# Modulation chunks summed over 1024 columns per VectorE operation, in pieces of 512 KB

## The chip, the cores and the metric

One core of one Trainium2 chip runs the kernel. The metric is device time in microseconds, the median of the timed runs. The engines are named as in the profile: PE is TensorE's matmul, PEld its weight load, DVE is VectorE, ACT is ScalarE, POOL is GpSimd, SP is the engine that issues most transfers.

## The reference, cut to what matters

The program is one layer of a hybrid backbone with width 2048 on 128 context tokens and 128 latent tokens, side by side as 256 columns:

```python
mod_ctx = (silu(c_ctx) @ w_mod + b_mod)      # 6 * 2048 values for the context tokens
mod_lat = (silu(c)     @ w_mod + b_mod)      # and 6 * 2048 for the latent tokens
shift1, scale1, gate1, shift2, scale2, gate2 = split(mod, 6)
h = rmsnorm(x) * (1 + scale1) + shift1
# h @ w_in feeds three branches: hgrn2 (a), chunk MLP (b), gated delta-net (c)
merged = g_a * (o_a @ w_br_hg) + g_b * (o_b @ w_br_cm) + g_c * (o_c @ w_br_gdn)
x = x + gate1 * (merged @ w_out)
h2 = rmsnorm(x) * (1 + scale2) + shift2
x = x + gate2 * (square(relu(h2 @ w_ff1)) @ w_ff2)
y = rmsnorm(x)
```

The modulation is a vector-matrix product, for two vectors, with a weight matrix of 2048 x 12288 fp32 values (96 MB). The kernel calls the six parts chunks 0 to 5. Chunks 0 and 1 are needed at the start; chunk 2 (`gate1`) after the output projection, chunks 3 and 4 at the second norm, chunk 5 (`gate2`) at the end.

## The kernel before

**The main stream.** All large products go through PE in units of one weight tile `[128, 1024]`, 512 KB each (`run_stream`, L388). SP loads a unit into a `raw` tile, ACT casts it to the high half `wh`, DVE subtracts to get the low half `wl` (`split`, L382), and PE multiplies three times: high by high, low by high, high by low. There are three `wh`/`wl` pairs in the steady state, so a split is made two units ahead of its use. Products accumulate in the PSUM banks `pb`; a block of 16 units gives four banks, which ACT or DVE empties.

**Fillers.** Everything else (normalizations, the three branches' inner work, modulation) is written as generators, the fillers. While it records the program, the kernel keeps a clock for each engine from a table of costs (`Meter.cost`, L123), and after each few matmuls `pump` (L300) lets fillers place their next instructions. A filler gets its turn when DVE and ACT are no more than `MARGIN` = 1.8 us ahead of PE by that clock. Small matmuls of fillers use the banks `pf` and stand between the main stream's. The recorded order is final: each engine runs its instructions in the order in which they were placed, and waits where an input is late. `finish` (L342) forces fillers out where the main stream needs their results; `gate` (L1451) calls it ahead of its evacuation for the branches that must be done by then, `gmlp` (L1337) among them for the second branch's gates. `norm_gate` (L787) closes the first and the third branch.

**The modulation.** Chunks 0 and 1 go through PE at the start. Chunks 2 to 5 are the background filler `mods` (L725), the last in the list, which gets a turn when DVE is less than `BG` = 0.8 us ahead of PE (L312). It puts output columns on the partitions: a piece of weights `mraw` is `[128, 512]`, 256 KB, with 512 of the 2048 inputs for 128 output columns. `cb` holds the matching quarter (`kq`) of both input vectors, copied to all partitions by a POOL transfer from the DRAM tile `csd`. For each of the two vectors one `scalar_tensor_tensor` multiplies the piece by `cb`, and its accumulated sum goes to one column of `part` (L757). Sixteen pieces make one quarter of a chunk; then `part` is added to `modc` (L761). There are three `mraw` buffers, and a piece is asked for two pieces ahead, on SP's queue, the same that carries the `raw` tiles. Chunk 5 starts only when the first block of `ff1` is done (`late`).

The chunks after the norm wait for `drain_mod` (L1673), which forces the background where a chunk is not complete. Tiles named `z` are large buffers that pass from one stage to the next.

Of the kernel before, what the change touches and what calls it, by code (L numbers as in the profile page):

```python
# [7 lines left out]
F32 = mybir.dt.float32  # L8
# [6 lines left out]
P = 128  # L15
D = 2048
KT = D // P
NB = 1024
# [174 lines left out]
class Backbone:  # L193
# [431 lines left out]
    def start_steps(self, first, second):  # L625
# [76 lines left out]
        for db in range(8):  # L702
            wins.append([dict(kind="call", do=lambda db=db: self.finish(self.chains[db])), first[2 * db]])
            wins += [[first[2 * db + 1]], [second[db]]]
        at = {8 * (g // 3 + 1) + (5, 7, 10)[g % 3]: w for g, w in enumerate(wins)}
        allm = sum(mods, [])
        for n in range(80):
            steps += allm[n:n + 1]
# [4 lines left out]
    def spread(self):  # L713

        nc = self.nc
        i, b = self.now(self.getbank())
        nc.tensor.transpose(b[:32, :P], self.cs.rearrange("p k v -> p (k v)"), self.ident)
        j, t = self.now(self.gettmp())
        nc.scalar.copy(t[:32, :P], b[:32, :P])
        self.putbank(i)  # L720
        self.csd = self.drp.tile([4, 8, P], F32, tag="csd", name="csd")
        nc.gpsimd.dma_start(self.csd.rearrange("a b p -> (a b) p"), t[:32, :P])
        self.puttmp(j)

    def mods(self, chs):  # L725


        nc = self.nc
        todo = [(ch, kq, n) for ch in chs for kq in range(4) for n in range(16)]
        raw, at = {}, {}  # L730

        def issue(m):
            if m < len(todo):
                ch, kq, n = todo[m]
                raw[m] = self.rawp.tile([P, 512], F32, tag="mraw", name=self.nm("mraw"))
                nc.sync.dma_start(raw[m], self.I["wmodr"][ch - 2, kq, n])
                at[m] = self.clock.dma + DMA1

        issue(0)
        issue(1)  # L740
        for m, (ch, kq, n) in enumerate(todo):
            yield 0.0
            while ch == 5 and not self.late:
                yield W
            if n == 0:
                cb = self.sp.tile([P, 4, 2, P], F32, tag="cb", name=self.nm("cb"))
                nc.gpsimd.dma_start(cb.rearrange("p a v j -> p (a v j)"), self.csd[kq].rearrange("a j -> (a j)").partition_broadcast(P))
                part = self.small(32, "part").rearrange("p (n v) -> p n v", n=16)
                yield W
            issue(m + 2)  # L750
            while not self.forced and at[m] > max(self.t["dve"], self.horizon()) + 0.2:
                yield W
            w = raw.pop(m).rearrange("p (a j) -> p a j", a=4)
            junk = self.junk.rearrange("p (v a j) -> p v a j", v=2, a=4)
            for v in range(2):
                nc.vector.scalar_tensor_tensor(out=junk[:, v], in0=w, scalar=1.0, in1=cb[:, :, v, :],
                                               op0=ALU.mult, op1=ALU.mult, accum_out=part[:, n, v:v + 1])  # L757
            if n < 15:
                continue
            c = self.modc[:, ch]  # L760
            nc.vector.tensor_tensor(out=c, in0=part, in1=self.bmod[:, ch].unsqueeze(2).broadcast_to([P, 16, 2]) if kq == 0 else c, op=ALU.add)  # L761
            if kq == 3:
                self.moddone.add(ch)


# [912 lines left out]
def _blocks(w, nb=NB):  # L1678

    k, n = w.shape  # L1680
    per = NB // nb
    w = w.reshape(k // P // per, per, P, n // nb, nb).transpose(3, 0, 2, 1, 4)
    return np.ascontiguousarray(w).reshape(n // nb, k // P // per, P, NB)


def _tail(w):

    return _blocks(w[:, :1024]), _blocks(w[:, 1024:1536], 512), _blocks(w[:, 1536:], 256)


def _cols(v):

    return v.reshape(-1, P).T


def layout(x_prompt, x_sample, c, state_hgrn, state_gdn, c_ctx, norm1_g, norm2_g, w_mod, b_mod, w_in,
           hg_lb, hg_onorm_g, cm_vnorm_g, cm_ws, cm_bs, gdn_conv, gdn_A_log, gdn_dt_bias, gdn_onorm_g,
           w_br_hg, w_br_cm, w_br_gdn, w_out, w_ff1, w_ff2, final_g):
    f = np.float32
    x = np.concatenate([x_prompt[0], x_sample[0]], 0)  # L1700
    A = {}
    A["xT"] = x.T.reshape(KT, P, 256).transpose(1, 0, 2)
    A["cvec"] = np.stack([_cols(c_ctx), _cols(c[0])], 2).reshape(P, 32)
    A["par"] = np.concatenate([b_mod[0].reshape(96, P).T, _cols(norm1_g[0]), _cols(norm2_g[0]), _cols(final_g),
                               _cols(hg_lb[0].reshape(-1)), hg_onorm_g[0][:, None], gdn_onorm_g[0][:, None],
                               _cols(cm_vnorm_g[0]),
                               gdn_conv[0].reshape(9, 24, P).transpose(2, 1, 0).reshape(P, 216),
                               np.zeros((P, 16), f)], 1)
    i = np.arange(P)
    A["ident"] = np.eye(P, dtype=f)  # L1710
    le, ge = i[:, None] <= i[None], i[:, None] >= i[None]
    lt, gt = i[:, None] < i[None], i[:, None] > i[None]
    A["tri"] = np.stack([le, ge, lt, gt], 1).astype(f)
    hm = np.zeros((P, 7, P), f)
    for j in range(7):
        m = 1 << j
        hm[:, j] = (i[:, None] // (2 * m) == i[None] // (2 * m)) & (i[:, None] // m != i[None] // m)
    A["hmask"] = hm
    A["sel"] = np.tile(np.eye(2, dtype=f), (2, 1))
    A["rows"] = np.concatenate([gdn_A_log[0].reshape(-1), gdn_dt_bias[0].reshape(-1)])  # L1720
    A["bs"] = cm_bs[0].reshape(-1)
    A["wsT"] = cm_ws[0].transpose(2, 0, 1)
    A["s0hg"] = state_hgrn[0, 0].transpose(2, 0, 1, 3)
    A["s0gd"] = state_gdn[0, 0].transpose(2, 0, 1, 3)
    wm = w_mod[0]
    m2 = wm[:, :2 * D].reshape(8, 2, P, 2, 8, 256)
    A["wmods"] = m2.transpose(4, 0, 2, 1, 3, 5).reshape(8, 8, P, NB)
    A["wmodr"] = wm[:, 2 * D:].reshape(4, 512, 4, KT, P).transpose(2, 0, 3, 4, 1)
    wi = w_in[0]

    o = {"hq": 0, "hi": 1024, "hgo": 2048, "hff": 3072, "hfb": 4096, "cu": 5120, "cv": 6144, "q": 7168, "k": 8192,
         "v": 9216, "ggo": 10240, "ab": 11264, "gates": 11296}
    starts = [o[n] for n in ("hi", "hff", "hff", "hq", "hgo", "q", "k", "v", "ggo", "cu", "cv")]
    starts += [o["gates"] + NB * j for j in range(6)]
    A["win"] = np.stack([wi[:, s:s + NB].reshape(KT, P, NB) for s in starts])
    hb = wi[:, o["hfb"]:o["hfb"] + NB].reshape(8, 2, P, 2, 512)
    A["winh"] = hb.transpose(3, 0, 2, 1, 4).reshape(2, 8, P, NB)
    A["wab"] = wi[:, o["ab"]:o["ab"] + 32].reshape(2, 8, P, 32).transpose(0, 2, 1, 3).reshape(2, P, 256)
    A["wbr"] = np.stack([_blocks(w[0]) for w in (w_br_hg, w_br_cm, w_br_gdn)])
    A["wouta"], A["woutb"], A["woutc"] = _tail(w_out[0])  # L1740
    A["wff1"] = _blocks(w_ff1[0])
    A["wff2"] = np.stack([_blocks(w_ff2[0][2048 * g:2048 * g + 2048]) for g in range(3)])
    A["wff2a"], A["wff2b"], A["wff2c"] = _tail(w_ff2[0][6144:])
    return {k: np.ascontiguousarray(v) for k, v in A.items()}
# [21 lines left out]
```

## Time and profile before

| | us |
|---|---|
| timed runs: median (lowest to highest) | 2031.3 (2029.57 to 2036.58) |
| the profiled execution | 2035.48 |
| its span, first to last instruction | 2033.7 |

```profile
## 2 busy tenths in 40 slices
PE   5999999999999989998999999899999999999997
...
DVE  6876898979878986877888856577887554455565
...
mraw<-in_wmodr SPq DMA_DIRECT2D x256, 256.0 KB, 4.0
...
cb<-csd POOLq DMA_DIRECT2D x16, 512.0 KB, 5.0
```

The page cuts the span into 40 slices of some 51 us; a digit is an engine's busy share in tenths. The last two lines count transfers with their size and the median time from issue to landing. In the tables by stretch further down, each engine has its busy time in that stretch with the number of its instructions, and then come the clock that TensorE was granted, the share of the DMA engines' time in use, and GB/s. In lists in order of time, the bracket is the idle time before an instruction and what ended it. Nearly all instructions carry line L169, that of the recording helper, so they are told apart by the names of their tiles.

### The profile page before, as it was taken

What the parts mean: (1) busy time and instruction counts of PE and PEld (TensorE: products, weight loads), DVE (VectorE), ACT (ScalarE), POOL (GpSimd) and SP (SyncE); (2) the same over time, 40 slices, a digit from 0 to 9 for tenths busy, and PEclk for the clock granted to TensorE, in tenths of its full rate; (3) what the DMA queues carried; (4) which work ended last, traced back from release to release, by engine and by line L of the source; (5) the groups of instructions that cost most, each with busy time, mean ns of one, the idle gap of its engine ahead of it and who ended that gap; (6) DMA issues with size and microseconds to landing.
All of it is one profiled execution on the core that took longest, in us unless ns stands there. A gap on an engine that the chain in (4) does not pass through costs nothing.

```text
span 2033.7 us, 35303 instructions
## 1 busy us (share of the span) xinstructions
PE 1967.6 (97%) x13749; PEld 1811.8 (89%) x13749; DVE 1489.7 (73%) x2662; ACT 1018.3 (50%) x1474; POOL 47.6 (2%) x117
## 2 busy tenths in 40 slices
PE   5999999999999989998999999899999999999997
PEld 3779988999888879886888899899999999999997
DVE  6876898979878986877888856577887554455565
ACT  6774645476647534475344434644444443344343
POOL 0000000000000001010000000000000000000000
PEclk9999999999999999999999999899999999999998
DMA  9886666665567765775888756577787555555654
GB/s 344 317 292 226 225 207 216 219 204 176 194 200 240 250 215 199 236 228 187 275 276 295 251 197 200 175 239 252 259 269 254 182 183 186 180 183 187 213 192 135
DMA packets 143040, 455.56 MB, mean 224 GB/s; under 512 B 16249, under 2 KB 16921, under 8 KB 141849
## 3 DMA queue, kind: packets, MB, share of 16 engines
q1 hardware_dynamic: 135216, 423.96, 62.5%
q0 software_dynamic: 7360, 29.07, 4.4%
q8 instruction: 108, 1.77, 0.3%
q14 instruction: 60, 0.48, 0.1%
q10 hardware_dynamic: 296, 0.27, 0.0%
HBM read 442.74 MB, written 10.50 MB: 223 GB/s over the span
## 4 chain that ended last, share of the span: by engine, by line
PE 85%; DVE 6%; DMA 5%; ACT 2%; issue 2%; POOL 0%; SPq 0%; DVEq 0%; ACTq 0%; POOLq 0%
PE pb L169 76%; PE pf L169 9%; DVE wl L169 2%; DVE z L169 2%; DVE m L169 1%; DMA z<-in_s0gd 1%; ACT wh L169 1%; DMA raw<-in_wmods 1%; DMA raw<-in_win 1%; DMA mraw<-in_wmodr 1%; DVE junk L169 1%; ACT z L169 1%; DMA raw<-in_winh 0%; ACT tp L169 0%; DMA z<-sp 0%
## 5 line engine op out<-in xcount | busy, mean ns | idle before, releaser
L169 DVE TENSOR_TENSOR wl<-raw,wh 128x1024 fp32r<-128x1024 f32 x610 | 742.6, 1221 | 455.3 <-ACT wh L169 454.1
L169 ACT CAST wh<-raw 128x1024 fp32r<-128x1024 f32 x610 | 637.2, 1047 | 826.9 <-PE pb L169 739.5
L169 PE MATMUL pb<-Hh,wh 128*128 128x256 f32 x2120 | 604.6, 285 | 7.5 <-ACT Hh L169 4.7
L169 PE MATMUL pb<-Hl,wh 128*128 128x256 f32 x2120 | 601.0, 284 | 0.8 <-DVE Hl L169 0.8
L169 PE MATMUL pb<-Hh,wl 128*128 128x256 f32 x2120 | 600.7, 283 | 0.0
L169 PEld LDWEIGHTS pb<-Hh,wh 128*128 128x128 f32 x2120 | 406.3, 192 | 10.3 <-ACT Hh L169 5.2
L169 PEld LDWEIGHTS pb<-Hl,wh 128*128 128x128 f32 x2120 | 406.2, 192 | 1.5 <-DVE Hl L169 1.4
L169 PEld LDWEIGHTS pb<-Hh,wl 128*128 128x128 f32 x2120 | 406.5, 192 | 0.9
L169 PE MATMUL pb<-z,wh 128*128 128x256 f32 x2048 | 367.3, 282 | 0.0
L169 DVE SCALAR_TENSOR_TENSOR junk<-mraw,cb 128x512 bf16<-128x512 f32 x512 | 329.3, 687 | 14.6 <-DMA mraw<-in_wmodr 10.9
L169 PEld LDWEIGHTS pb<-z,wh 128*128 128x128 f32 x2048 | 317.2, 190 | 0.0
L169 PE MATMUL pb<-z,wl 128*128 128x256 f32 x1024 | 289.2, 282 | 0.1
L169 PE MATMUL pb<-wh,Hh 128*128 128x512 f32 x640 | 258.5, 404 | 3.3 <-DVE z L169 3.0
L169 PE MATMUL pb<-wl,Hh 128*128 128x512 f32 x640 | 250.4, 391 | 1.3 <-DVE wl L169 1.3
L169 PE MATMUL pb<-wh,Hl 128*128 128x512 f32 x640 | 250.3, 391 | 0.0
L169 PEld LDWEIGHTS pb<-z,wl 128*128 128x128 f32 x1024 | 195.0, 190 | 0.3 <-DVE wl L169 0.3
L169 PEld LDWEIGHTS pb<-wh,Hh 128*128 128x128 f32 x640 | 120.7, 189 | 28.6 <-DVE z L169 3.9
L169 PEld LDWEIGHTS pb<-wh,Hl 128*128 128x128 f32 x640 | 120.6, 188 | 25.8
L169 PEld LDWEIGHTS pb<-wl,Hh 128*128 128x128 f32 x640 | 120.9, 189 | 24.4 <-DVE wl L169 2.4
L169 PE MATMUL pb<-wh,z 128*128 128x512 f32 x384 | 123.9, 399 | 4.5 <-ACT z L169 4.5
L169 PEld LDWEIGHTS pb<-wh,z 128*128 128x128 f32 x384 | 73.1, 191 | 21.1 <-ACT z L169 5.3
L169 PE MATMUL pb<-wl,z 128*128 128x512 f32 x192 | 76.0, 396 | 0.0
(174 smaller groups left out, 1595.8 us busy)
## 6 DMA issues: line engine op xcount, KB each, us to landing
raw<-in_win SPq DMA_DIRECT2D x249, 512.0 KB, 3.8
raw<-in_wff SPq DMA_DIRECT2D x224, 512.0 KB, 3.6
mraw<-in_wmodr SPq DMA_DIRECT2D x256, 256.0 KB, 4.0
raw<-in_wbr SPq DMA_DIRECT2D x48, 512.0 KB, 3.5
z<-in_wmods SPq DMA_DIRECT2D x39, 512.0 KB, 5.8
raw<-in_wmods SPq DMA_DIRECT2D x25, 512.0 KB, 6.0
cb<-csd POOLq DMA_DIRECT2D x16, 512.0 KB, 5.0
raw<-in_wouta SPq DMA_DIRECT2D x16, 512.0 KB, 3.5
```

The costliest lines, as they stand in the source:

```text
L169: return f(*a, **k)
```

## The change

A piece is now `[128, 1024]`, 512 KB, with 1024 inputs for 128 output columns. There are two values of `kq` in place of four, so a chunk takes 32 pieces and not 64. One `scalar_tensor_tensor` sums over 1024 columns; both vectors' products go to the same `junk` tile. `cb` has twice the size, and is loaded 8 times in place of 16. To make room in SBUF the descriptor scratch of POOL's transfers is set to 4096 bytes. The weights are laid out for it on the host.

```diff
-        self.csd = self.drp.tile([4, 8, P], F32, tag="csd", name="csd")
+        self.csd = self.drp.tile([2, 16, P], F32, tag="csd", name="csd")
...
-        todo = [(ch, kq, n) for ch in chs for kq in range(4) for n in range(16)]
+        todo = [(ch, kq, n) for ch in chs for kq in range(2) for n in range(16)]
...
-                raw[m] = self.rawp.tile([P, 512], F32, tag="mraw", name=self.nm("mraw"))
+                raw[m] = self.rawp.tile([P, NB], F32, tag="mraw", name=self.nm("mraw"))
...
-                cb = self.sp.tile([P, 4, 2, P], F32, tag="cb", name=self.nm("cb"))
+                cb = self.sp.tile([P, 8, 2, P], F32, tag="cb", name=self.nm("cb"))
...
-            w = raw.pop(m).rearrange("p (a j) -> p a j", a=4)
-            junk = self.junk.rearrange("p (v a j) -> p v a j", v=2, a=4)
+            w = raw.pop(m).rearrange("p (a j) -> p a j", a=8)
+            junk = self.junk.rearrange("p (a j) -> p a j", a=8)
             for v in range(2):
-                nc.vector.scalar_tensor_tensor(out=junk[:, v], in0=w, scalar=1.0, in1=cb[:, :, v, :],
+                nc.vector.scalar_tensor_tensor(out=junk, in0=w, scalar=1.0, in1=cb[:, :, v, :],
                                                op0=ALU.mult, op1=ALU.mult, accum_out=part[:, n, v:v + 1])
...
-            if kq == 3:
+            if kq == 1:
                 self.moddone.add(ch)
...
-    A["wmodr"] = wm[:, 2 * D:].reshape(4, 512, 4, KT, P).transpose(2, 0, 3, 4, 1)
+    A["wmodr"] = wm[:, 2 * D:].reshape(2, NB, 4, KT, P).transpose(2, 0, 3, 4, 1)
...
-    nc = _bacc.Bacc("TRN2", target_bir_lowering=False, num_devices=1)
+    nc = _bacc.Bacc("TRN2", target_bir_lowering=False, num_devices=1, dynamic_dma_scratch_size=4096)
```

The planner sees other lengths, so it places the fillers of the whole middle of the program differently: PE has the same 12561 rows in both, but from the 916th on the small matmuls stand elsewhere. Three places follow, each before and after.

The first is DVE where modulation begins, just behind the start of the main projection (`x2` is the pair for the two vectors). Before:

```order
L169 SCALAR_TENSOR_TENSOR junk,part_1700<-mraw_1791,cb_1698 128x512 x2
L169 SCALAR_TENSOR_TENSOR junk,part_1700<-mraw_1801,cb_1698 128x512 x2
L169 TENSOR_TENSOR wl_1904<-raw_1809,wh_1903 128x1024
L169 SCALAR_TENSOR_TENSOR junk,part_1700<-mraw_1835,cb_1698 128x512 x2
L169 TENSOR_TENSOR wl_1938<-raw_1841,wh_1937 128x1024
L169 SCALAR_TENSOR_TENSOR junk,part_1700<-mraw_1899,cb_1698 128x512 x2
L169 TENSOR_TENSOR wl_1972<-raw_1871,wh_1971 128x1024
L169 SCALAR_TENSOR_TENSOR junk,part_1700<-mraw_1933,cb_1698 128x512 x2
```

The same place after:

```order
L169 SCALAR_TENSOR_TENSOR junk,part_1700<-mraw_1809,cb_1698 128x1024 x2
L169 TENSOR_TENSOR wl_1900<-raw_1833,wh_1899 128x1024
L169 SCALAR_TENSOR_TENSOR junk,part_1700<-mraw_1825,cb_1698 128x1024 x2
L169 TENSOR_TENSOR wl_1934<-raw_1839,wh_1933 128x1024
L169 SCALAR_TENSOR_TENSOR junk,part_1700<-mraw_1883,cb_1698 128x1024 x2
L169 TENSOR_TENSOR wl_1968<-raw_1869,wh_1967 128x1024
```

Between two splits there still stands about one piece, but it is a pair of twice the width.

The second is DVE at the end of `gmlp`, just ahead of branch(1,0), the product that uses its result. `wl_9428` and `wl_8913` are splits of that product's second unit; `z_1362` and `z_1249` hold gmlp's values, `tp` its spatial weights; `z_1455` and `z_1339` take the low halves that the product reads. `z_1389` is the low half of the delta-net branch's closing norm. Before:

```order
L169 TENSOR_TENSOR wl_9428<-raw_9346,wh_9427 128x1024
L169 SCALAR_TENSOR_TENSOR z_1389_9076<-pf_9407,par,z_1388_9075 128x512
L169 SCALAR_TENSOR_TENSOR z_1389_9076<-pf_9412,par,z_1388_9075 128x512
L169 SCALAR_TENSOR_TENSOR z_1389_9076<-pf_9447,par,z_1388_9075 128x512
L169 SCALAR_TENSOR_TENSOR z_1389_9076<-pf_9452,par,z_1388_9075 128x512
L169 SCALAR_TENSOR_TENSOR z_1362_8968<-pf_9460,par,tp_9378 128x2x128 x2
L169 TENSOR_TENSOR z_1362_8968<-z_1362_8968,z_1226_8232 128x2x2x128
L169 SCALAR_TENSOR_TENSOR z_1362_8968<-pf_9466,par,tp_9381 128x2x128 x2
L169 TENSOR_TENSOR z_1455_9478<-z_1362_8968,z_1454_9477 128x512 x4
```

After:

```order
L169 SCALAR_TENSOR_TENSOR z_1249_8386<-pf_8852,par,tp_8764 128x2x128 x2
L169 TENSOR_TENSOR z_1249_8386<-z_1249_8386,z_1157_7875 128x2x2x128
L169 TENSOR_TENSOR z_1153_7858<-z_1153_7858,pf_8857 128x256
L169 TENSOR_TENSOR wl_8877<-raw_8789,wh_8876 128x1024
L169 SCALAR_TENSOR_TENSOR junk,part_8455<-mraw_8809,cb_8453 128x1024 x2
L169 TENSOR_TENSOR wl_8913<-raw_8817,wh_8912 128x1024
L169 TENSOR_TENSOR z_1339_8892<-z_1249_8386,z_1338_8891 128x512 x2
L169 TENSOR_TENSOR m_1247_8368<-m_1247_8368,pf_8900 128x512
L169 TENSOR_TENSOR z_1339_8892<-z_1249_8386,z_1338_8891 128x512 x2
```

What stood in one lump behind the split, the closing norm included, is now only the low halves; gmlp's last part has moved ahead of two splits and one piece.

The third is PE where the delta-net's second half reads the cached states, which POOL loads into `z_1144`, `z_1146` before and `z_1155`, `z_1168` after (two chains that run side by side). Before:

```order
L169 MATMUL pf_7729<-z_1144_7615,z_665_4190 128x128 x4
L169 MATMUL pf_7736<-z_1146_7629,z_665_4190 128x128 x4
L169 MATMUL pb_7453<-Hh_242,wh_7637 128x256
L169 MATMUL pb_7453<-Hh_242,wl_7638 128x256
L169 MATMUL pb_7453<-Hl_243,wh_7637 128x256
```

After:

```order
L169 MATMUL pf_7925<-z_1155_7861,z_633_4064 128x128 x4
L169 MATMUL pb_7889<-wh_7833,Hh_242 128x512
L169 MATMUL pb_7889<-wl_7834,Hh_242 128x512
L169 MATMUL pb_7889<-wh_7833,Hl_243 128x512
L169 MATMUL pb_7886<-wh_7880,Hh_242 128x512
L169 MATMUL pb_7886<-wl_7881,Hh_242 128x512
```

Before, both chains read at once; after, the second chain's first read (of `z_1168`) stands 29 rows behind the first's.

## The prediction

> **What bounds the kernel now.** I read the totals first, then busy time in stretches, then the waits of the engine that is busy nearly all the time, and then the order of instructions where those waits lie.
>
> ```profile
> span 2033.7 us, 35303 instructions
> PE 1967.6 (97%) x13749; PEld 1811.8 (89%) x13749; DVE 1489.7 (73%) x2662; ACT 1018.3 (50%) x1474; POOL 47.6 (2%) x117
> ```
>
> PE (TensorE) sets the time: it is busy for 1967.6 of 2033.7 us, and the change leaves its instructions alone, the same number before and after. So VectorE (DVE) work that goes is worth nothing by itself; only PE's 66 idle us, and pieces at a reduced clock, can be won, and only as far as DVE or a transfer causes them. Stretches of 50 us say where they are (PE busy, PEld, DVE, ACT, POOL, granted PE clock, DMA share, GB/s):
>
> ```profile
> 0.00:50.00 50.00, 28.24 (x125) 15.37 (x126) 31.04 (x39) 33.27 (x44) 1.96 (x7) 0.97 0.93 346
> ...
> 250.00:300.00 50.00, 50.00 (x266) 42.97 (x265) 48.73 (x91) 23.09 (x29) 1.46 (x2) 1.00 0.59 191
> ...
> 700.00:750.00 50.00, 47.17 (x268) 41.30 (x267) 48.13 (x91) 21.64 (x26) 1.82 (x3) 1.00 0.59 185
> ...
> 900.00:950.00 50.00, 43.62 (x213) 35.22 (x212) 37.66 (x72) 32.62 (x90) 4.99 (x9) 1.00 0.70 221
> ...
> 1050.00:1100.00 50.00, 50.00 (x222) 41.42 (x221) 42.89 (x85) 21.15 (x23) 1.06 (x2) 1.00 0.86 284
> 1100.00:1150.00 50.00, 49.22 (x215) 40.05 (x214) 40.70 (x84) 21.00 (x22) 0.00 (x0) 1.00 0.87 297
> ...
> 1400.00:1450.00 50.00, 50.00 (x419) 50.00 (x418) 43.02 (x82) 22.00 (x25) 0.00 (x0) 1.00 0.78 257
> ```
>
> The first 50 us lose 21.8 us of PE before any modulation piece is read; they stay, and so does the tail. In the two stretches where DVE is fullest, PE loses nothing once (250) and 2.8 us once (700): a full DVE can hurt but need not. The place to look is 900 to 960. In steps of 5 us:
>
> ```profile
> 935.00:940.00 5.00, 3.79 (x21) 2.82 (x20) 5.00 (x7) 1.92 (x3) 1.07 (x2) 1.00 0.85 234
> 940.00:945.00 5.00, 3.31 (x18) 2.20 (x16) 4.13 (x9) 1.39 (x3) 0.00 (x0) 1.00 0.80 272
> 945.00:950.00 5.00, 2.05 (x16) 1.86 (x16) 4.21 (x8) 0.47 (x2) 0.00 (x0) 1.00 0.10 38
> 950.00:955.00 5.00, 2.86 (x6) 1.66 (x6) 2.50 (x4) 3.94 (x7) 0.00 (x0) 0.51 0.00 0
> 955.00:960.00 5.00, 5.00 (x19) 3.97 (x19) 2.50 (x3) 3.48 (x6) 0.00 (x0) 0.80 0.06 9
> ```
>
> PE idles 8.0 us here, and its clock is down to 0.51 and 0.80 behind it (2.86 x 0.49 + 5.00 x 0.20 = 2.4 us): 10.4 us in all. What it waits for is in order of time, PE, ACT and DVE apart (start, length, operation, and in brackets the idle time before it with its releaser):
>
> ```profile
> 943.37 1.29 PE L169 MATMUL pf<-ident,z 128*128 128x128 f32 x8 [1.32 <-DVE z L169]
> 945.56 2.05 PE L169 MATMUL pf<-tp,z 128*128 128x128 f32 x16 [0.90 <-DVE z L169]
> 952.14 0.79 PE L169 MATMUL pb<-wh,z 128*128 128x512 f32 x1 [4.52 <-ACT z L169]
> ```
> ```profile
> 949.91 2.18 ACT L169 CAST z<-z 128x512 fp32r<-128x512 f32 x4 [4.53 <-DVE z L169]
> ```
> ```profile
> 946.76 0.88 DVE L169 SCALAR_TENSOR_TENSOR z<-pf,par,tp 128x256 f32<-128x256 f32 x2 [0.59 <-PE pf L169]
> 947.67 0.69 DVE L169 TENSOR_TENSOR z<-z,z 128x512 f32<-128x512 f32 x1
> ```
>
> This is `finish` in `gate` (L1453): the spatial-gating branch `gmlp` was not done when the weights of gate(1,0) were used up, so its last two parts, with half of the delta-net branch's closing `norm_gate`, are forced out with PE standing.
>
> **The change, part by part.** *DVE work.* One piece is now one pair of 1024-column sums in place of two pairs of 512. What they cost is the distance between starts, since a sum's end overlaps its successor:
>
> ```profile
> 1403.94 0.69 DVE L169 SCALAR_TENSOR_TENSOR junk<-mraw,cb 128x512 bf16<-128x512 f32 x1
> 1404.55 0.08 DVE L169 DVE_READ_ACCUMULATOR junk<-mraw,cb 128x1 f32 x1
> 1404.55 0.69 DVE L169 SCALAR_TENSOR_TENSOR junk<-mraw,cb 128x512 bf16<-128x512 f32 x1
> ```
> ```profile
> 648.25 2.35 DVE L169 TENSOR_TENSOR wl<-raw,wh 128x1024 fp32r<-128x1024 f32 x2
> 650.52 1.22 DVE L169 STREAM_TRANSPOSE m<-z 32x32 f32<-32x32 f32 x8
> ```
>
> 512 columns take 0.614 us; a product without a sum of 1024 takes (650.52 - 648.25) / 2 = 1.135. A 1024-column sum isn't in the trace: at least 1.135 (that product), at most 2 x 0.614 = 1.23; I take 1.15, from the nearer row. So DVE goes from 512 x 0.614 = 314 us to 256 x 1.15 = 294: **20 us less, on an engine that is off the path**, hidden by PE's dense matmuls. Half of the final additions go too, some 8 tiny rows.
>
> *Order.* The planner starts a background piece when DVE is less than 0.8 us ahead of PE, however long the piece is. With pieces of 2.3 us in place of 1.23 it gets more modulation in per unit of weights. Counted in the order by the weight splits (`wl` rows) between: chunks 2 to 4 take 225 splits where they took 282, chunk 5 some 52 where it took 78. Other fillers wait longer behind a piece, and the delta-net chain ends later. Both matter:
>
> Term 1, the stall at 935. Now gmlp's four parts come out one by one inside gate(1,0), and no norm_gate row is near. Behind the last gmlp matmul group stand 28 wide matmuls and two groups of four small ones (by the 1050 row 50 / 222 = 0.225 us for a wide one, by the 945.56 row 2.05 / 16 = 0.13 for a small one: 7.3 us) before the branch's first one. DVE has to do 0.88 + 0.69 (rows above), some 0.35 for a half-width sum, 1.14, a piece of 2.3, 1.14 and the first 512 columns of the low halves, 0.61 like a sum of that width, in that time: 7.1. That is about even, so I leave 1 us of stall, and the clock should stay up. **-9.4 us**; ends -10.4 (nothing left) and -4 (DVE arrives late behind that piece).
>
> Term 2, the refill behind it. The transfers ran dry at 950 and came back at once:
>
> ```profile
> 966.56 0.69 DVE L169 SCALAR_TENSOR_TENSOR junk<-mraw,cb 128x512 bf16<-128x512 f32 x1 [1.13 <-DMA mraw<-in_wmodr]
> ...
> 975.00 0.69 DVE L169 SCALAR_TENSOR_TENSOR junk<-mraw,cb 128x512 bf16<-128x512 f32 x1 [1.03 <-DMA mraw<-in_wmodr]
> ```
> ```profile
> 975.00:980.00 5.00, 3.71 (x17) 2.75 (x16) 5.00 (x12) 1.47 (x2) 0.00 (x0) 1.00 0.76 241
> ```
>
> Without the standstill there is no such burst, and two pieces ahead are now 4.6 us of DVE work rather than 2.5. **-1.3 us**; the other end is 0.
>
> Term 3, the cached states. Two delta-net chains read them at the same moment, PE waiting 1.22 and 2.52 us, with the clock at 0.74 for 2.82 busy us (0.7):
>
> ```profile
> 758.53 1.13 PE L169 MATMUL pf<-z,z 128*128 128x128 f32 x8 [1.22 <-DMA z<-in_s0gd]
> 762.18 1.84 PE L169 MATMUL pf<-z,z 128*128 128x128 f32 x8 [2.52 <-DMA z<-in_s0gd]
> ```
> ```profile
> 760.00:765.00 5.00, 2.82 (x14) 2.85 (x15) 3.86 (x13) 0.00 (x0) 0.00 (x0) 0.74 0.88 302
> ```
>
> In the new order the second chain's reads stand some 29 PE rows behind the first's, the four transfers still together. I drop part of the second wait: **-2 us**; ends -4.4 (both gone, clock too) and +2 (a bigger piece ahead in the queues delays all four).
>
> Term 4: modulation for chunks 3 and 4 is over before 1000 us, so the 0.78 us that PE loses in the 1100 stretch goes: **-0.8**; the other end 0.
>
> Term 5, what a fuller DVE costs elsewhere. In chunk 5's stage 52 splits now share DVE with 32 pieces: 52 x 1.14 + 32 x 2.3 + 24 squares x 0.61 = 147 us, while PE needs 52 x 24 x 0.119 = 149 (50 / 419 by the 1400 row). DVE is full for three stretches of 50 us, and about 7% fuller in chunks 2 to 4. By the 250 row that costs 0, by the 700 row 2.8 us a stretch, some 10 with the earlier stage; below nothing, -4, if waits on DVE in the later, wider spaced delta-net steps shrink. I take **+3**, since the 1400 row, from the same stage, loses nothing.
>
> Nothing else is on the path: 128 fewer DMA issues on SP, 8 fewer copies of `cb` of twice the size on POOL, the same bytes. The smaller descriptor scratch touches only POOL's transfers; those show a steady time to issue:
>
> ```profile
> L169 POOL DMA_DIRECT2D z<-in_s0gd x4: 719/719/724, 749.6 to 792.2; - x4
> L169 POOL DMA_DIRECT2D z<-sp x8: 531/558/655, 749.1 to 866.2; - x8
> ```
>
> I cost it at nothing; its upper end is in term 3.
>
> Sum: -9.4 - 1.3 - 2.0 - 0.8 + 3.0 = -10.5. The profiled execution took 2035.5 us (span 2033.7), so 2025.0 on its terms. The timed runs' median, 2031.3, is 4.2 lower. PE's terms that I touch are about a quarter of its idle time, so I let them be 1 us smaller in the median run: 2031.3 - 9.5, some **2022 us**.
>
> The Trainium skill, TensorE: Matmul & The Clock Gate, Part 1, lets the clock halve after an idle window of about 3.4 us. The 0.51 behind 4.52 us agrees; the 0.74 behind waits of at most 2.52 does not, and by the page term 3 would have no clock part and be 0.7 us smaller at its far end. Its page SBUF — State Buffer, section SBUF: two separate sides, says that a DVE instruction with two SBUF inputs can hold GpSimd out of a shared port until it ends, which speaks against longer sums. The POOL rows above spread by 0.12 us at most with a DVE at 73%, so I see no such block; by the page each of the 12 transfers for the delta net could start up to 0.53 us later, and term 3 would come to -2 + 12 x 0.53 = +4.4.
>
> **Rivals.** *A. The stall only moves.* Idle on PE goes at 935, but the delta-net chain, now spread over gates (1,0) and (1,1), makes PE wait at its own steps, or chunk 5's full DVE does. For it: the 700 row, and the chain's last steps stand six matmuls apart. Against: DVE has no modulation left there. Terms 1 and 2 stay, 3 is 0, and 5 goes to +7: 2031.3 - 4.5, some 2027. That is within 0.3%, about the least that a measurement of this kernel can tell from no change.
>
> *B. The change does not reach PE.* DVE's 20 us were covered, and gmlp comes late all the same because the 2.3 us piece stands just ahead of its low halves: 2031 plus or minus 3. For it: DVE's and PE's times to the branch are even within 0.2 us.
>
> The third rival needs the cast that comes before each split (1047 ns):
>
> ```profile
> L169 ACT CAST wh<-raw 128x1024 fp32r<-128x1024 f32 x610 | 637.2, 1047 | 826.9 <-PE pb L169 739.5
> ```
>
> *C. Slower.* DVE runs too far ahead of PE with fillers, and the next split comes late. A split for the unit after next has two units, 2 x 24 x 0.119 = 5.7 us, less the ACT cast (1.05) and itself (1.14): 3.5 us of room. A piece of 1.23 and a filler step of four 512-wide operations (2.4) just fit; 2.3 + 2.4 = 4.7 is 1.2 over. It decides when this meets in more than 8 of the 128 pieces, which eats the gain; in 16 it costs 19, giving 2041. Against: the planner counts the longer piece, and stops at 1.8 us of lead for other fillers.
>
> **How the numbers follow.** Forecast 0.58, A and B 0.28 together, C 0.14. Lower end: terms at -10.4 - 1.3 - 4.4 - 0.8 - 4 make -21, or 2010 on the median; 2011 leaves out only all of them at once. Upper end: all of A and B, and C up to half of its 10 us, 2036. The bound of 0.3% is 6.1 us: faster means below 2025.2, slower above 2037.4. Chances: faster 0.58, same 0.28, slower 0.14.
>
> **What would show it.** DVE sums of 1024 starting 1.15 us apart and DVE busy near 1470 us; PE idle between the last gmlp group and branch(1,0) of 1 us or less with the clock at 1.00; the two chains' first reads apart; PE at 50.00 in the chunk 5 stretches with DVE at 48 or more. I am wrong if PE idles over 1 us a stretch there, or if rows of `wl` end late in the chunk 2 to 4 stage.

## The result, and the profile after

| | median, us | lowest to highest |
|---|---|---|
| before | 2031.41 | 2029.57 to 2036.58 |
| after | 2043.49 | 2042.42 to 2048.87 |

The change makes the kernel slower: ratio 1.006, 95% interval [1.0041, 1.0079], some 12 us. That is above the forecast range, and the other sign. The profiled execution of after took 2048.87 us (span 2047.1), the one of before 2035.48.

The page of after, lines as shown of before:

```profile
span 2047.1 us, 34444 instructions
...
PE 1977.8 (97%) x13749; PEld 1818.4 (89%) x13749; DVE 1475.3 (72%) x2142; ACT 1019.1 (50%) x1476; POOL 43.2 (2%) x109
...
DVE  6876999989888988988364556598964554455565
...
PE 69%; DVE 15%; issue 6%; DMA 6%; ACT 4%; SPq 0%; DVEq 0%; POOL 0%; ACTq 0%; POOLq 0%
...
mraw<-in_wmodr SPq DMA_DIRECT2D x128, 512.0 KB, 5.5
...
cb<-csd POOLq DMA_DIRECT2D x8, 1024.0 KB, 7.7
```

DVE has 14.4 us less to do, and yet its share of the chain that ended last is 15%. In the profile of before that row of the chain reads:

```profile
PE 85%; DVE 6%; DMA 5%; ACT 2%; issue 2%; POOL 0%; SPq 0%; DVEq 0%; ACTq 0%; POOLq 0%
```

So an engine with less to do has become a larger part of that chain. Where, the stretches of after show (columns as in the prediction):

```profile
650.00:700.00 50.00, 47.28 (x221) 39.33 (x220) 49.37 (x94) 26.08 (x51) 2.15 (x4) 1.00 0.77 268
700.00:750.00 50.00, 44.38 (x215) 37.09 (x214) 44.03 (x86) 26.86 (x47) 3.77 (x7) 1.00 0.78 272
...
900.00:950.00 50.00, 45.25 (x238) 37.48 (x238) 44.69 (x67) 20.68 (x31) 3.19 (x9) 0.97 0.71 239
950.00:1000.00 50.00, 50.00 (x310) 43.89 (x308) 30.04 (x40) 23.87 (x45) 4.83 (x16) 1.00 0.60 195
1100.00:1150.00 50.00, 50.00 (x221) 41.28 (x221) 22.88 (x19) 20.98 (x22) 0.00 (x0) 1.00 0.62 197
1350.00:1400.00 50.00, 49.70 (x414) 49.50 (x413) 49.40 (x70) 20.76 (x24) 0.00 (x0) 1.00 0.82 283
1400.00:1450.00 50.00, 46.87 (x373) 46.16 (x372) 42.49 (x58) 21.07 (x25) 0.53 (x1) 0.97 0.79 278
```

From 900 to 1000 PE gained, as forecast, though less. From 650 to 750 it loses 8.3 us, and in chunk 5's stage, at 1400, it loses 3.1 where it lost nothing before. Before, 650 to 750 lost 4.6: 2.8 in the 700 row that the prediction shows, and 1.7 in this one:

```profile
650.00:700.00 50.00, 48.26 (x233) 40.40 (x232) 48.94 (x121) 27.48 (x56) 4.33 (x8) 1.00 0.78 263
```

To compare whole runs I take, for each matmul of a trace, the distance to the next one's start less the median for its shape, and add these up by stage: PE's **excess** in us, waits and slow clock in one.

| stage, us | 0–200 | 200–550 | 550–900 | 900–1000 | 1000–1300 | 1300–1550 | rest | all |
|---|---|---|---|---|---|---|---|---|
| before | 18.0 | 1.9 | 21.6 | 14.3 | 11.7 | -0.9 | 3.2 | 69.8 |
| after | 22.6 | 4.7 | 25.6 | 8.8 | 11.8 | 6.3 | 4.4 | 84.0 |

The 14.2 us of difference agree with the 13.4 between the two profiled executions.

Next, DVE in order of time in after, at one of the stalls (666 us) and at the sums themselves:

```profile
662.65 1.23 DVE L169 TENSOR_TENSOR wl<-raw,wh 128x1024 fp32r<-128x1024 f32 x1
663.79 1.22 DVE L169 SCALAR_TENSOR_TENSOR junk<-mraw,cb 128x1024 bf16<-128x1024 f32 x1
...
665.05 1.22 DVE L169 SCALAR_TENSOR_TENSOR junk<-mraw,cb 128x1024 bf16<-128x1024 f32 x1
...
666.20 2.48 DVE L169 TENSOR_TENSOR z<-pb,z 128x512 f32<-128x512 f32 x4
```

```profile
666.94 0.50 PE L169 MATMUL pb<-wh,Hh 128*128 128x512 f32 x1 [2.72 <-DVE z L169]
```

Two things are to be seen. A whole piece, 2.41 us, stands between a split and the emptying of PE's banks (`z<-pb`), and PE waits 2.72 us for the first bank. And the second sum starts 1.26 us after the first, while what follows starts 1.15 after it: the pair takes 2.41, not 2.30. Both sums write the same `junk` tile, and in the built program the second waits on DVE's own semaphore; before, each vector had its half of `junk`, and no sum waits on the one just before it.

### The profile page after: what moved, and what is told of

It is laid out like the page before. It is cut to its first block, busy times and chain, and to the rows that moved or that the text cites. A ratio compares the mean times of both kernels' runs of the same rounds, so it can differ in the third digit from the quotient of the medians.

```text
span 2047.1 us, 34444 instructions
## 1 busy us (share of the span) xinstructions
PE 1977.8 (97%) x13749; PEld 1818.4 (89%) x13749; DVE 1475.3 (72%) x2142; ACT 1019.1 (50%) x1476; POOL 43.2 (2%) x109
## 4 chain that ended last, share of the span: by engine, by line
PE 69%; DVE 15%; issue 6%; DMA 6%; ACT 4%; SPq 0%; DVEq 0%; POOL 0%; ACTq 0%; POOLq 0%
PE pb L169 63%; PE pf L169 7%; DVE wl L169 6%; DVE z L169 4%; DVE junk L169 3%; DMA mraw<-in_wmodr 2%; ACT wh L169 2%; DVE m L169 1%; DMA raw<-in_wff 1%; ACT z L169 1%; DMA raw<-in_winh 1%; ACT tp L169 1%; DMA raw<-in_wmods 1%; ACT L169 0%; DMA z<-in_s0gd 0%
## 5 line engine op out<-in xcount | busy, mean ns | idle before, releaser
L169 DVE SCALAR_TENSOR_TENSOR junk<-mraw,cb 128x1024 bf16<-128x1024 f32 x256 | 312.9, 1222 | 7.3 <-DMA mraw<-in_wmodr 2.7
```

The lines of the kernel that those rows point to most:

```text
L169: return f(*a, **k)
```

## The experiments

Ratios are to the kernel before on the same chip, with their 95% interval. "Step" is what the background places in one turn.

**The wait between the sums, and two other suspects.** e1 gives the two sums of the change their own halves of `junk`. e2 lowers the bound for background work in the change. e3 is the kernel before with the change's small descriptor scratch. e4 is the kernel before with its sums sharing one half of `junk`.

```diff
e1, against the change
-        self.junk = c("junk", [P, 1024], mybir.dt.bfloat16)
+        self.junk = c("junk", [P, 2048], mybir.dt.bfloat16)
-            junk = self.junk.rearrange("p (a j) -> p a j", a=8)
+            junk = self.junk.rearrange("p (v a j) -> p v a j", v=2, a=8)
-                nc.vector.scalar_tensor_tensor(out=junk, in0=w, ...
+                nc.vector.scalar_tensor_tensor(out=junk[:, v], in0=w, ...
e2, against the change
-BG = 0.8
+BG = -0.35
e3, against before
-    nc = _bacc.Bacc("TRN2", target_bir_lowering=False, num_devices=1)
+    nc = _bacc.Bacc("TRN2", target_bir_lowering=False, num_devices=1, dynamic_dma_scratch_size=4096)
e4, against before
-                nc.vector.scalar_tensor_tensor(out=junk[:, v], in0=w, ...
+                nc.vector.scalar_tensor_tensor(out=junk[:, 0], in0=w, ...
```

> The changed kernel, but the two vectors' products go to separate halves of a junk tile of twice the size; every engine's order stays as in the changed kernel. In the changed kernel the second sum of a pair starts 1.26 us after the first, the next instruction 1.15 us after that: it waits for the first one's write to the same junk tile, 0.11 us in each of 128 pairs, 14 us of DVE. Theory W (that wait uses up what the longer sums save, and makes DVE late for splits and evacuations): pairs at 2.30 us, chunk 5's stage without PE waits, 2043 falls by 6 to 12 us, to 2031 to 2037. Theory L (the lump of a whole piece ahead of splits and evacuations is what costs, 2.3 or 2.4 us alike): pairs at 2.30 us too, but under 3 us gained, 2040 or more. Theory S (the smaller descriptor scratch): no gain.

> The changed kernel, but a background piece starts only when DVE is 0.35 us behind PE by the planner's clock (BG = -0.35 in place of 0.8), so that after a piece of 2.3 us DVE is as far ahead as it was after a piece of 1.2 us before the change. The junk tile stays shared. Theory L: PE waits on DVE's evacuations (2.9 to 3.0 us at 664, 718 and 746 us) shrink by about 1 us each and the stage of chunk 5 loses nothing: 2030 to 2036. Theory W: pairs stay at 2.41 us, but DVE has slack between them, so it gains too, some 3 to 6 us, 2037 to 2040. Theory S: no gain.

> The kernel before with the descriptor scratch of POOL's transfers at 4096 bytes and nothing else changed; the order is that of the kernel before. Theories W and L: 2031, within 0.2%. Theory S: slower by several us, up to 2043, with longer POOL issues than 531 to 719 ns, or transfers of the cached states that land later than 8.7 us.

> The kernel before, but both 512-column sums of a pair write the same half of the junk tile; the order is that of the kernel before. Theory W: each second sum starts 0.11 us later, 256 times, 28 us more of DVE, which the slack of a DVE at 73% takes up in part: 2034 to 2045. Theories L and S: DVE's 28 us are covered, 2031 to 2034.

e1: 1.0018 [1.0004, 1.0031], 2036.03 us. e2: 1.038 [1.0364, 1.0397]. e3: 1.0006 [0.9995, 1.0018]. e4: 1.0035 [1.0022, 1.0048]. The order of e1 is that of the change, that of e3 and e4 that of before. The wait is priced by rows of DVE in order of time, a pair and the instruction behind it in e1, and then three sums of 512 columns in e4:

```profile
1423.12 1.22 DVE L169 SCALAR_TENSOR_TENSOR junk<-mraw,cb 128x1024 bf16<-128x1024 f32 x1
...
1424.26 1.22 DVE L169 SCALAR_TENSOR_TENSOR junk<-mraw,cb 128x1024 bf16<-128x1024 f32 x1
...
1425.41 1.22 DVE L169 TENSOR_TENSOR wl<-raw,wh 128x1024 fp32r<-128x1024 f32 x1
```

```profile
1410.00 0.69 DVE L169 SCALAR_TENSOR_TENSOR junk<-mraw,cb 128x512 bf16<-128x512 f32 x1
...
1410.72 0.69 DVE L169 SCALAR_TENSOR_TENSOR junk<-mraw,cb 128x512 bf16<-128x512 f32 x1
...
1411.46 0.69 DVE L169 SCALAR_TENSOR_TENSOR junk<-mraw,cb 128x512 bf16<-128x512 f32 x1
```

With two halves the pair takes 2.29; with one, a sum of 512 columns takes 0.73 in place of 0.614. So sharing `junk` makes some 0.4 points of the change's 0.6, and costs the kernel before 0.35. The scratch does nothing that can be told. e2 was a miss: modulation came so late that PE stood still from 1300 to 1350 while it was forced out.

**Place, step length and grain.** e5 is the kernel before with its tiles where e1's stand. e6 is e1 with a point between the two sums where other work may come in. e7 keeps the 512 KB pieces and the 1 MB `cb`, but sums 512 columns at a time, with a point in the middle of a piece. e8 is e1 with the background held while `gmlp` places its low halves.

```diff
e5, against before (cb and junk likewise at twice their size, and the small scratch)
-                raw[m] = self.rawp.tile([P, 512], F32, tag="mraw", name=self.nm("mraw"))
+                raw[m] = self.rawp.tile([P, NB], F32, tag="mraw", name=self.nm("mraw"))[:, :512]
e6, against e1 (behind a sum)
+                if v == 0:
+                    yield 0.0
e7, against the change (w is cut into two halves h; part has a column for each)
-            for v in range(2):
-                nc.vector.scalar_tensor_tensor(out=junk, in0=w, ... in1=cb[:, :, v, :], ...
+            for h in range(2):
+                for v in range(2):
+                    nc.vector.scalar_tensor_tensor(out=junk[:, v], in0=w[:, h], ... in1=cb[:, 4 * h:4 * h + 4, v, :], ...
+                if h == 0:
+                    yield 0.0
e8, against e1 (hold is set in gmlp after its products, and cleared at its end)
-            while ch == 5 and not self.late:
+            while self.hold or ch == 5 and not self.late:
                 yield W
```

> The kernel before, in its own order and with its own sums, but its tiles stand in SBUF where those of the change with two junk halves stand: each piece is loaded into the first half of a tile twice as wide, cb likewise, junk has twice the columns, the descriptor scratch is 4096. Theory P (place): PE loses more from 100 to 200 us in each kernel with the new layout (8.8 to 10.2 us, against 5.4 to 5.7 in the three profiles with the old one), although the instructions there are the same ones in the same order; if the addresses do it, this run loses 8 to 10 us there and the ratio to the kernel before is 1.0010 to 1.0025. Theory N (it lies in what modulation asks for from 175 us on, or is chance): 5 to 6 us there, ratio 1.000 within 0.001.

> The change with two junk halves, and the planner may put other work between the two 1024-column sums of a piece. Theory L (a whole piece of 2.3 us in front of a split or an evacuation makes PE wait): the waits at 664, 718 and 746 us, 2.4 to 2.6 us each with two halves, fall to 1.4 or less, and the three at 918 to 925 us likewise; 4 to 6 us less than with whole pieces, ratio to the kernel before 0.999 to 1.000. Theory W alone (all the harm was the wait between the sums, which is gone already): as with whole pieces, 1.0018 within 0.001.

> The 512 KB pieces and the 1 MB cb stay, but each piece is summed in two halves of 512 columns, two sums each as in the kernel before, with a point between them where other work may come in: DVE work and its grain as before, transfers as in the change. Theory L (grain of DVE work): PE's loss from 600 to 750 us comes back from 11.5 to about 6.6 us, ratio 0.999 to 1.001. Theory D (grain of the transfers: a load of 512 KB or 1 MB in front of the weights): the loss stays, ratio 1.002 to 1.004.

> The change with two junk halves, and modulation holds still from the end of gmlp's last product until its low halves are placed: the piece between the two splits ahead of them goes behind them. Theory T (the wait of 4 us that stays at 918 to 925 us is that piece, and PE needs all four low halves and not the first only): that wait falls to 1.5 us or less, 2.5 us in all, ratio 1.0005 within 0.001. Rival: the first of these waits is on the ACT casts, which end at 919.7, and the piece that goes later makes a split late there: nothing gained, 1.0018.

e5: 1.0002 [0.9987, 1.0018]; the place is nothing. e6: 0.9975 [0.9958, 0.9993], 0.4 points under whole pieces and more than theory L had. e7: **0.9937** [0.9919, 0.9956], 2024.31 us. e8: 0.9997 [0.9981, 1.0012]. e7 was faster than any theory had it, with every transfer of the change in place, so the big loads alone do not do the harm; but its sums, its steps and its order all differ from e1's, which left the cause open. e8 puts the piece behind the low halves, and PE's waits at that place come to about 1 us:

```profile
910.91 1.22 DVE L169 TENSOR_TENSOR wl<-raw,wh 128x1024 fp32r<-128x1024 f32 x1
912.04 1.29 DVE L169 TENSOR_TENSOR z<-z,z 128x512 fp32r<-128x512 f32 x2
...
916.40 1.22 DVE L169 SCALAR_TENSOR_TENSOR junk<-mraw,cb 128x1024 bf16<-128x1024 f32 x1
```

```profile
916.54 0.73 PE L169 MATMUL pb<-wh,z 128*128 128x512 f32 x2 [0.18 <-DVE z L169]
918.53 0.50 PE L169 MATMUL pb<-wh,z 128*128 128x512 f32 x1 [0.80 <-ACT z L169]
```

But e8 had 4.8 us of excess from 1300 to 1550, where e1 had 0.8, though neither has the wait between the sums. So that stage is not explained by the wait alone; the section on why the prediction was wrong comes back to it.

**Depth, and the luck of the order.** e9 is the kernel before with six buffers of 256 KB and pieces asked for five ahead; it has the small scratch too, as have e14 and e15. e10 is e7 with a piece asked for only one ahead. e11 is e7 with e8's hold. e12 is the kernel before with `BG` = 1.0: the same work in another order.

```diff
e9, against before
-                raw[m] = self.rawp.tile([P, 512], F32, tag="mraw", name=self.nm("mraw"))
+                raw[m] = self.rawp.tile([P, 512], F32, tag="mraw", name=self.nm("mraw"), bufs=6)
-        issue(0)
-        issue(1)
+        for m in range(5):
+            issue(m)
-            issue(m + 2)
+            issue(m + 5)
e10, against e7
-        issue(1)
-            issue(m + 2)
+            issue(m + 1)
e12, against before (e15 against e9, e16 against the change)
-BG = 0.8
+BG = 1.0
```

> The kernel before with six buffers for its 256 KB pieces and five asked for ahead: as many bytes ahead as with 512 KB pieces, sums and cb as before. Theory A (what made the 512 KB pieces with 512-column sums fast, 0.9937, is that more is loaded ahead): 0.993 to 0.997. Theory C (it is that cb is reloaded 8 times and not 16, each reload stopping modulation): 1.000 within 0.0015, since in the order chunk 4 is done after 330 splits, where it was 342 before and 303 with the fast kernel.

> The kernel with 512 KB pieces and 512-column sums, but a piece is asked for only one ahead: 512 KB ahead as in the kernel before, cb still reloaded 8 times. Theory A (depth): back to 1.000 within 0.0015. Theory C (reloads of cb): 0.9937 stays, within 0.002. In its order chunk 4 is done after 336 splits, as in the kernel before.

> The kernel with 512 KB pieces and 512-column sums, and modulation held still from the end of gmlp's last product until its low halves are placed. If a piece stands ahead of those in this order too, 1 us less than 0.9937 gives; else the order hardly moves and the ratio is the same, 0.993 to 0.994. Both theories of the speed leave it below 0.996.

> The kernel before with nothing changed but the bound for background work, 1.0 us in place of 0.8: another order of the same instructions with the same transfers. It shows how far an arbitrary change of the order moves the time. Theory O (differences of some 0.3% between these kernels are the luck of where the fillers fall): a ratio off by 0.002 or more to either side. Otherwise 1.000 within 0.001, and the ratios of the other kernels tell of their sums and pieces.

e9: **0.9932** [0.9914, 0.9950]. e10: 0.9963 [0.9948, 0.9979], between its two theories. e11: 0.9942 [0.9923, 0.9960]; its order had little to hold. e12: 1.0024 [1.0011, 1.0037]. The last is a yardstick: a mere other order is worth a quarter of a per cent, so single differences of that size between kernels with different orders prove nothing. From here on pairs decide.

**Long steps, and other orders.** e13 is e7 without its point in the middle: four sums of 512, 2.46 us, in one step. e14 is e9 with a turn only after every second piece, also 2.46. e15 is e9, and e16 the change, each with `BG` = 1.0.

```diff
e13, against e7
-                if h == 0:
-                    yield 0.0
e14, against e9
-            yield 0.0
+            if n % 2 == 0:
+                yield 0.0
```

> The fast kernel (512 KB pieces, sums of 512 columns, 0.9937) without the point in the middle of a piece: its four sums, 2.46 us, are one step again. Theory L (the length of one background step): back to 1.001 to 1.004, as with two sums of 1024 (1.0018). Theory S (sums of 1024 columns are worse in themselves, not the step): 0.994 to 0.996. Theory O (only luck of the order): anywhere from 0.994 to 1.004, and e14 says otherwise than this.

> The kernel before with six buffers (0.9932), where the planner gets a turn only after every second piece: a step of 2.46 us, loads of 256 KB as before. Theory L: 1.001 to 1.004. Theory D (the load of 512 KB in front of the weights): 0.993 to 0.995.

> The kernel before with six buffers and a bound of 1.0 us in place of 0.8: another order, the same pieces and loads. Theory A (more loaded ahead is worth it): at least 0.004 under the kernel before with 1.0 (1.0024), so 0.992 to 0.998. Theory O (its 0.9932 is the luck of one order): 0.999 or more.

> The changed kernel with a bound of 1.0 us: another order of the same work. Theories W and L (its loss is its own): 1.004 to 1.009 of the kernel before, 1.002 to 1.006 of that one with 1.0. Theory O: the sign may turn, 1.002 or less.

e13: 0.9989 [0.9977, 1.0002]. e14: 0.9994 [0.9983, 1.0005]. e15: 0.9937 [0.9924, 0.9950]. e16: 1.0033 [1.0019, 1.0047]. A step of twice the length costs 0.5 points with large loads and 0.6 with small ones, so it is the step and not the transfer; the forecast of 1.001 and more for both was too high. The gain of six buffers holds in another order: 0.9932 against 1, and 0.9937 against 1.0024.

The loss of the change does not hold in the same way. The partner of e16 is e12, and 1.0033 / 1.0024 = 1.0009, with intervals that overlap: with this bound the change can't be told from the kernel before. e16 met neither forecast against the kernel before (it is under 1.004 and over 1.002), and against e12 it is under the 1.002 that theories W and L had at least. So the 0.6% is what the change cost in one order, and its size is in part that order's luck. What shows in both orders is a loss in chunk 5's stage, 5.9 us of excess from 1300 to 1550 in e16 against -0.9 in e12, and a gain from 900 to 1000, 3.9 against 11.7.

**The planner's price.** For a sum of 1024 columns `Meter.cost` (L123) gives 0.07 + 1024 x 0.00104 = 1.135 us, so a pair counts 2.27, and takes 2.41. e17 is the change, one `junk` tile and the waits included, with 1.205 for a sum. PE, ACT, SP and POOL then have, row for row, the order of e13. e18 adds the point between the two sums, and has the order of e7 in the same way. So e17 differs from e13, and e18 from e7, in DVE's sums alone.

```diff
e17, against the change
+        if "accum_out" in k and n == 1024:
+            c += 0.07
         return c
e18, against e17 (behind a sum)
+                if v == 0:
+                    yield 0.0
```

> The changed kernel, with one junk tile and its waits, but the planner's cost of a 1024-column sum is 1.205 us in place of 1.135, so that a pair counts 2.41, what it takes. PE, ACT, SP and POOL then have the same order as in the run with four 512-column sums as one step (0.9989). Theory M (the wait harms because the plan counts on 2.27, puts in a piece more than DVE can do, chunk 5 above all: 52 splits for its 32 pieces, now 56): 0.997 to 1.001, and PE loses nothing to speak of from 1300 to 1550. Theory W (the time of the wait itself, or sums of 1024 columns in themselves): 1.003 to 1.006.

> The same with a point between the two sums where other work may come in: the order of the fast kernel with 512-column sums (0.9937), with the change's 1024-column sums. Theory M with L (only the plan's count and the length of the step matter): 0.992 to 0.996. Theory S (1024-column sums cost PE something of their own): 0.997 or more.

e17: **0.9979** [0.9966, 0.9992], 2030.70 us. e18: **0.9939** [0.9921, 0.9957], 2022.46 us. Chunk 5's stage in e17, in stretches of 50 us:

```profile
1350.00:1400.00 50.00, 50.00 (x419) 50.00 (x418) 47.65 (x64) 22.48 (x26) 0.00 (x0) 1.00 0.82 283
1400.00:1450.00 50.00, 50.00 (x419) 50.00 (x419) 45.99 (x63) 22.02 (x25) 0.53 (x1) 1.00 0.82 291
1450.00:1500.00 50.00, 50.00 (x423) 50.00 (x422) 49.32 (x67) 22.76 (x26) 0.00 (x0) 1.00 0.84 286
```

PE is full, with a DVE that is about as full as in after. And in the same order two long sums with the wait do as well as four short ones without it: 0.9979 beside e13's 0.9989, and, for e18, 0.9939 beside e7's 0.9937.

The chain that ended last in e18:

```profile
PE 87%; DVE 5%; issue 3%; DMA 2%; ACT 2%; POOL 0%; SPq 0%; DVEq 0%; ACTq 0%; POOLq 0%
```

Two small edits to the plan thus turn the change from 0.6% slower into 0.6% faster than before, with its pieces, its sums and its waits all kept. The excess of the kernels that matter, by stage:

| stage, us | 0–200 | 200–550 | 550–900 | 900–1000 | 1000–1300 | 1300–1550 | rest | all |
|---|---|---|---|---|---|---|---|---|
| e1, own halves | 24.2 | 2.5 | 23.5 | 8.2 | 11.7 | 0.8 | 3.3 | 74.1 |
| e17, told the price | 21.8 | 5.1 | 19.5 | 7.5 | 11.5 | -0.9 | 3.2 | 67.8 |
| e18, and a half step | 18.0 | 1.7 | 18.8 | 3.6 | 9.4 | -0.9 | 3.7 | 54.3 |
| e9, six small buffers | 20.6 | 2.1 | 18.6 | 4.4 | 11.9 | -0.9 | 3.6 | 60.3 |

## Why the prediction was wrong

**The step that failed is term 5, "what a fuller DVE costs elsewhere", taken at +3 us.** It came to some 22: by the two excess rows 0–200 rose by 4.6, 200–550 by 2.8, 1300–1550 by 7.2 and the end by 1.2, and within 550–900 the part up to 750 rose by 6.5 (11.3 to 17.8). Of this the first 4.6 lie almost wholly ahead of the first modulation piece; profiles differ there by as much (e18: as before), and I leave it open. The rest has two causes. By e16 and e12 its total is that of one order; the causes are read from pairs of runs.

*The price.* It took 1.15 us for a sum, from a product without a sum, and did not ask what the second sum waits for, although the diff drops the halves of `junk`. With 2.41 a pair, chunk 5's stage needs 52 x 1.14 + 32 x 2.41 + 24 x 0.61 = 151 us of DVE beside 149 of PE, where the prediction had 147: it is over, not just under. In the 5 us steps of after:

```profile
1435.00:1440.00 5.00, 2.70 (x21) 2.30 (x20) 5.00 (x8) 4.50 (x6) 0.00 (x0) 1.00 0.26 99
1440.00:1445.00 5.00, 5.00 (x31) 5.00 (x31) 4.20 (x6) 0.84 (x1) 0.00 (x0) 0.66 0.80 257
```

PE stands for 2.3 us beside a DVE that works without a break, and pays again with a clock of 0.66. The 1400 row of before, on which the +3 rested, says little here, since there chunk 5 was spread over 78 splits. (The prediction also took 250 and 700 for the stretches with the fullest DVE; the 650 row of before is fuller, 48.94, and loses 1.7. That would have moved its estimate little.)

DVE was not without a break just ahead of that stall. ACT, and DVE behind it:

```profile
1422.91 1.05 ACT L169 CAST wh<-raw 128x1024 fp32r<-128x1024 f32 x1 [5.18 <-DMA raw<-in_wff]
```

```profile
1423.99 2.51 DVE L169 TENSOR_TENSOR wl<-raw,wh 128x1024 fp32r<-128x1024 f32 x2 [5.01 <-ACT wh L169]
```

A weight load is asked for when DVE's split has freed its tile (SP's queue waits 48.4 us for splits from 1380 to 1450), and this one ran beside `cb`'s reload of 1 MB (asked for at 1414.4, 7.6 us to landing). From 1350 to 1500 ACT waits for weight loads 35.3 us in after, 29.2 in e8, 24.8 in e1 and 30.2 in e17, and not at all in before. So the stall is made of a full DVE and of late loads, and no run divides the two; but e17 has the loads nearly as late and loses nothing.

What harms is that the plan does not know the price. Against rival C the prediction set that "the planner counts the longer piece"; it counts 2.27 for 2.41, and so places chunk 5 within 52 splits, where with the true price it takes 56. In e17 and e18 DVE has the same pairs with the same waits, and in this stage the loss of the change is gone. e1 takes away the other side of the same difference: 52 splits without the wait lose 0.8. But e8, with 52 splits and no wait either, loses 4.8; so 52 splits leave too little room even at 2.29 a pair, and whether that costs anything depends on the order. Since e17 and the change also differ in order, a part of their 0.8 points may be the order's luck, of which e12 shows 0.24.

*The step.* "Other fillers wait longer behind a piece" stood in the prediction, and only two places were priced. Three pairs price it all over: e7 to e13, e9 to e14 and e18 to e17, 0.4 to 0.6 points or 8 to 13 us. The orders differ within each pair, and the first and the third share theirs; but all three have the same sign, at about twice what e12 shows for an order alone. PE then waits not so much for splits, as rival C had it, as for emptied banks (666 us above) and for values that a branch reads. After's waits of PE from 550 to 900 (total in us, times, longest) have no `wl` among them. Before has 4.6 and 0.3 in the first two rows, and e18 2.6 and none:

```profile
PE pb L169 <- DVE z L169: 5.4, 2, 2.7
PE pb L169 <- ACT z L169: 4.5, 2, 2.9
PE pf L169 <- issue: 2.0, 1, 2.0
PE pf L169 <- DMA z<-in_s0gd: 1.2, 1, 1.2
PE pf L169 <- DVE m L169: 0.9, 1, 0.9
```

**Term 1, -9.4, and term 2, -1.3,** were right in kind: gmlp's forced lump is gone, and 900 to 1000 gained 5.5 of the 10.7. Here is the place in after in order of time, DVE and then PE:

```profile
917.01 0.87 DVE L169 SCALAR_TENSOR_TENSOR z<-pf,par,tp 128x256 f32<-128x256 f32 x2
...
919.99 1.22 DVE L169 SCALAR_TENSOR_TENSOR junk<-mraw,cb 128x1024 bf16<-128x1024 f32 x1
...
922.41 1.22 DVE L169 TENSOR_TENSOR wl<-raw,wh 128x1024 fp32r<-128x1024 f32 x1
923.54 1.28 DVE L169 TENSOR_TENSOR z<-z,z 128x512 fp32r<-128x512 f32 x2
924.75 0.68 DVE L169 TENSOR_TENSOR m<-m,pf 128x512 f32<-128x512 f32 x1
925.35 1.29 DVE L169 TENSOR_TENSOR z<-z,z 128x512 fp32r<-128x512 f32 x2
```

```profile
923.08 0.50 PE L169 MATMUL pb<-wh,z 128*128 128x512 f32 x1 [0.49 <-ACT z L169]
926.69 0.74 PE L169 MATMUL pb<-wh,z 128*128 128x512 f32 x2 [2.87 <-DVE z L169]
928.65 0.80 PE L169 MATMUL pb<-wh,z 128*128 128x512 f32 x1 [0.78 <-ACT z L169]
```

The sum of 7.1 us for DVE counted "the first 512 columns of the low halves". PE waited for all four, and one `m` row stood among them: 926.6 - 917.0 = 9.6. Hence 4.1 us of waits and not 1. e8, which moves the piece behind, brings them to 1.

**Term 3, -2:** right. 750 to 900 gained 2.5 (10.3 to 7.8), and of the waits for the cached states one of 1.2 us is left (the `in_s0gd` row above).

**Term 4, -0.8:** the 1100 row is at 50.00 as forecast, but 1000 to 1300 as a whole gained nothing, since a wait of like size came at 1038.

**DVE's saving** was 14.4 us, not 20, and worth nothing, as said: e18 and e7 have the same order, and the same time. **The scratch** cost nothing, as said (e3), and POOL's issues for the cached states took 717 to 724 ns beside the longer sums, 719 to 724 before.

**Rival A** named the right places for a loss, the delta-net steps and chunk 5's full DVE, and gave them +7; 550 to 750 and 1300 to 1550 came to some 14. **Rival B** had its reason in part: the piece just ahead of the low halves costs PE some 3 us, by e8. **Rival C** had the sign and the engine, and with 2041 nearly the time. PE did wait for splits in chunk 5's stage, but for 2.4 us and not 19, so that nearness is luck.

Not in the prediction at all: that six small buffers, with more bytes asked for ahead, are worth some 0.7 points (e9) and 0.9 (e15 against e12). Why is shown only in part. In the profile of e9, 900 to 1000 has 4.4 us of excess where before has 14.3; but e10, which asks for no more bytes ahead than before, has that as well (1.9), so the larger `cb` or the order may do it too.

## What to carry to other kernels

Where a planner places work by a table of costs, measure the pair as it will run, waits on the engine's own results included, and put that into the table: here one entry was 6% off (2.27 for 2.41), and with the true figure the kernel went from 0.6% slower to 0.2% faster, some of which may be the order's luck. Work that fills gaps should come in steps shorter than the slack of what waits behind it. And before a difference of some tenths of a per cent is explained, run both kernels in an arbitrary other order: six buffers kept their gain in it, and the change did not keep its loss.

## What the hardware showed beyond what was expected

An accumulating sum that waits on the DVE sum just before it starts 0.11 to 0.12 us later than one that does not: 1.26 against 1.15 us behind a sum of 1024 columns, 0.73 against 0.614 behind one of 512. The Trainium skill, VectorE: DVE Perf Modes, section The DRAIN you can't avoid, has eight copies with a semaphore after each take the same time as with one at the end, so that a semaphore costs nothing extra; for these accumulating sums the rows say otherwise, and the measurement decides.

PE's clock fell to 0.66 in the stretch behind 1435, where its waits in the whole of 1400 to 1450 were these (total, times, longest):

```profile
PE pb L169 <- DVE wl L169: 2.4, 2, 1.6
PE pb L169 <- ACT wh L169: 0.7, 1, 0.7
```

So two waits that together make some 2.3 us within 5 stood ahead of it, none longer than 1.6. The length of a wait does not settle it: behind the 2.72 us at 666 the clock stayed at 1.00 (the 650 row of after).
